# Three plain gate pairs instead of four in an FFN, and low halves written by adding DMAs

## The chip, the cores and the metric

One core of one Trainium2 chip runs the whole program in one launch. The metric is the device time of a launch in microseconds (us). TensorE is called PE below, its weight loads PEld, VectorE DVE, ScalarE ACT, GpSimd POOL, SyncE SP. ACT, POOL and SP can also issue DMAs.

## The reference, cut to what matters

The program is one inference step of a two-layer decoder for 512 prompt positions and 8 x 4 sample positions, 544 columns in all. Each layer has a half-step FFN, a mixer, a cross-attention and a second half-step FFN. The change concerns the four FFNs alone:

```
def _swiglu(x, wg, wu, wd):
    return (jax.nn.silu(x @ wg) * (x @ wu)) @ wd

x = x + 0.5 * _swiglu(_rmsnorm(x, n[0]), P['f1_wg'][l], P['f1_wu'][l], P['f1_wd'][l])
...
x = x + 0.5 * _swiglu(_rmsnorm(x, n[3]), P['f2_wg'][l], P['f2_wu'][l], P['f2_wd'][l])
```

x has 1024 features, the hidden layer 2816, all in float32.

## The kernel before

**Halves.** The kernel wants more precision than one matmul in PE's fast float32 format (fp32r) gives. So every operand is split: hi is the value rounded to fp32r by an ACT copy, lo is value minus hi, by a DVE subtraction. A product is three matmuls: hi weights by hi x, hi weights by lo x, lo weights by hi x (`TERMS`). In `dense` each is done for two halves of 272 columns, so the fifth matmul of a product is the first that reads the lo weights.

**Plain gates and pairs.** The 2816 hidden columns are 11 blocks ("pairs") of 256. A pair's product can be done in two ways. The plain way is two gates (`gate`) of 8 x 3 x 2 = 48 matmuls. The other way is a 2 x 2 block scheme with seven products instead of eight (`p1` to `p7` in `run`, 7 x 4 x 3 = 84 matmuls); it needs sums of weight blocks (the tile `sb` is made by two plain loads on SP and one adding DMA on POOL, in `sums`; `ga_s` makes two more sums on DVE), and sums and differences of x (`forms`). A group of products needs its own split weights: al (for p1 and p2), be (p5, p7), ga (p6, p3), de (p4), made by functions such as `al_h` (ACT copy) and `al_l` (DVE subtraction).

**Stages of an FFN.** In part 0 of three, the gate matrix `wg` of pairs 0 to 3 is done by eight plain gates, while DVE and ACT make the x forms; then `wu` of the same pairs by the seven products; then the partial down projection. Parts 1 and 2 do `wg` and `wu` both by the seven products. The plain gates work on x before its normalisation, whose factor `rstd` is multiplied in when a gate is evicted from PSUM (tile g); the forms need the normalised x, so they can't begin until `rstd` is there. Four calls of `forms`, one for each two chunks of x, follow gates 2, 3, 4 and 5.

**Order.** It is written out by hand: `step` collects functions, and `emit_steps` calls them one after the other; each engine runs its own instructions in that order. Ahead of a step, `conv` makes the split weights for up to the third gate in the list (`la=3`), from a raw buffer (two of these, `rawp`) into a wc buffer (three, `wcp`). When the last unit of a raw buffer is converted, `release` calls `issue`, which lets SP load the next block. The preparation of the first pair (`prelude`) stands ahead of the last gate. In the first FFN (`hold`), the first two gates start before anything else of the program and the factor comes after gate 1; in the others it comes after gate 0.

Two places in the code carry the rest. The conversion's DVE part, and the order in part 0:

```
        def low():
            tt(pool if u.on_pool else dve, w[:, 1], src, w[:, 0].bitcast(F32), ALU.subtract)
            if not u.raw:
                release(u)
...
                    if c == 7:
                        step(lambda P=items[0]: prelude(P))
                    step(lambda u, c=c: gate(u, c), us[j])
                    if c in (2, 3, 4, 5):
                        step(lambda kp=c - 2: forms(kp))
```

`actv` (L92), `tt` (L86), `stt` (L89) and `mm` (L95) are helpers, so many instructions carry one of these line numbers; the matmuls of the seven products carry L391.

Of the kernel before, what the change touches and what calls it, by code (L numbers as in the profile page):

```python
# [7 lines left out]
F32 = mybir.dt.float32  # L8
F32R = mybir.dt.float32r
AF = mybir.ActivationFunctionType  # L10
ALU = mybir.AluOpType
# [18 lines left out]
class Unit:  # L30
    def __init__(self, blk, k0, nk, c0, nc):
        self.blk, self.k0, self.nk, self.c0, self.nc = blk, k0, nk, c0, nc
        self.on_pool = self.late = self.raw = self.manual = False


class Block:
# [12 lines left out]
def trunk_kernel(ctx, tc, I, O):  # L49
    nc = tc.nc  # L50
    pe, act, dve, pool, sp = nc.tensor, nc.scalar, nc.vector, nc.gpsimd, nc.sync
# [11 lines left out]
    def nm(s):  # L63
        cnt[0] += 1
        return f"{s}{cnt[0]}"
# [10 lines left out]
    def P2(n="ps"):  # L76
        return PS(n), PS(n)
# [4 lines left out]
    def ph(ps, i):  # L82
        return ps[i][:, 0:HT]

    def tt(e, out, a, b, op):
        e.tensor_tensor(out=out, in0=a, in1=b, op=op)  # L86
# [4 lines left out]
    def actv(out, a, f, **kw):  # L91
        act.activation(out=out, in_=a, func=f, **kw)  # L92
# [13 lines left out]
    def step(fn, *units, la=3, ahead=None):  # L106
        steps.append((fn, units, la, ahead))
# [18 lines left out]
    def emit_steps():  # L126
        order = []
        for _, us, _, _ in steps:
            order.extend(us)
        blks = []  # L130
        for u in order:
            if u.blk not in blks[-3:]:
                blks.append(u.blk)
        st = {"dma": 0, "conv": 0}

        def issue(part=0):
            if part:
                b = blks[0]
                h = b.nk // 2
                sp.dma_start(out=b.tile[:, h:], in_=b.ap[:, h:])  # L140
                return
            if st["dma"] >= len(blks):
                return
            b = blks[st["dma"]]
            st["dma"] += 1
            b.tile = rawp.tile([128, b.nk, b.nc], F32, tag="raw", name=nm("raw"))
            if b.extra:
                sp.dma_start(out=b.tile, in_=b.ap)
                b.extra(b)
            elif st["dma"] == 1:  # L150
                h = b.nk // 2
                sp.dma_start(out=b.tile[:, 0:h], in_=b.ap[:, 0:h])
            else:
                sp.dma_start(out=b.tile, in_=b.ap)

        def release(u):
            u.blk.left -= 1
            if u.blk.left == 0:
                issue()

        def conv(defer=None):
            u = order[st["conv"]]
            st["conv"] += 1
            if u.manual:
                return
            w = wcp.tile([128, 2, u.nk, u.nc], F32R, tag="wc", name=nm("wc"))
            src = u.blk.tile[:, u.k0:u.k0 + u.nk, u.c0:u.c0 + u.nc]
            actv(w[:, 0], src, AF.Copy)
            u.tile = w

            def low():
                tt(pool if u.on_pool else dve, w[:, 1], src, w[:, 0].bitcast(F32), ALU.subtract)
                if not u.raw:
                    release(u)
            if defer is None or not u.late:
                low()
            else:
                defer.append(low)

        S["release"] = release  # L180
        startup(C_NORM, issue, conv)
        used = 0
        for fn, us, la, ahead in steps:
            used += len(us)
            flush()
            post = []
            while ahead is not None and st["conv"] < min(len(order), used + ahead):
                conv()
            while us and st["conv"] < min(len(order), used - len(us) + la):
                conv(post)  # L190
            fn(*us)
            for f in post:
                f()
            for u in us:
                if u.raw:
                    release(u)
        while later or waiting:
            flush()
# [15 lines left out]
    def split(hi, lo, src, delay=True):  # L214
        actv(hi, src, AF.Copy)

        def f():
            tt(dve, lo, src, hi.bitcast(F32), ALU.subtract)
        if delay:
            later.append(f)  # L220
        else:
            f()

    def sumsq(c):
        if c == 0:
# [68 lines left out]
    def ffn(which, l, next_g, tail=None):  # L294
        wg, wu = I[which + "_wg"][l], I[which + "_wu"][l]
        gcol = C_NORM + (l * 4 + (3 if which == "f2" else 0)) * 8
        G, XF, hh, hl = {}, {}, {}, {}
        hold = l == 0 and which == "f1"
        held = []
        kmap = [(z, 2 * (z % 4) + 1 - z // 4) for z in (4, 0, 5, 1, 6, 2, 7, 3)]  # L300

        def gate(u, c):
            ps = P2("gps")
            dense(ps, u, xh, xl, kmap)
            held.append((ps, c))
            if c == 7:
                for k in range(KD):
                    xh[k] = xl[k] = None
            if hold and c == 0:
                return  # L310
            if c == int(hold):
                norm_end()
            for ps, c in held:
                for i in range(2):
                    if c % 2 == 0:
                        G[c // 2, i] = U([128, 2, HT], n="g")
                    tt(dve, G[c // 2, i][:, c % 2], ph(ps, i), hb(S["rstd"], i), ALU.mult)
                if c % 2:
                    for i in range(2):
                        actv(G[c // 2, i], G[c // 2, i], AF.Silu)  # L320
            held.clear()
            if c == 7:
                S["rstd"] = S["ss"] = None

        def forms(kp):
            xs = D([128, 2, NT], n="xs")
            v = xs.rearrange("p a (h t) -> p (a h) t", h=2)
            t1, t2 = U([128, 2, HT], n="xt"), U([128, 2, HT], n="xt")
            b = U([128, 2, HT], F32R, n="xb")
            hs, ls = ([U([128, 2, HT], F32R, n="xf") for z in range(3)] for y in range(2))  # L330
            for j in range(2):
                stt(xs[:, j], x[2 * kp + j], col(gcol + 2 * kp + j), S["rstd"], ALU.mult, ALU.mult)
            actv(b[:, 0], v[:, 0], AF.Copy)
            actv(hs[0], v[:, 2:4], AF.Copy)
            tt(dve, t1, v[:, 0:4:3], v[:, 1:2].to_broadcast([128, 2, HT]), ALU.subtract)
            actv(hs[1], t1, AF.Copy)
            stt(t2[:, 0], t1[:, 0], -1.0, v[:, 3], ALU.mult, ALU.subtract)
            tt(dve, b[:, 1], v[:, 0], b[:, 0].bitcast(F32), ALU.subtract)
            stt(t2[:, 1], t2[:, 0], -1.0, v[:, 2], ALU.mult, ALU.subtract)
            actv(hs[2], t2, AF.Copy)  # L340
            for z, src in enumerate((v[:, 2:4], t1, t2)):
                tt(dve, ls[z], src, hs[z].bitcast(F32), ALU.subtract)
            XF[1, kp] = (b[:, 0], b[:, 1])
            for i, z, a in ((2, 0, 0), (3, 0, 1), (5, 1, 0), (7, 1, 1), (6, 2, 0), (4, 2, 1)):
                XF[i, kp] = (hs[z][:, a], ls[z][:, a])
# [119 lines left out]
        def pair(w, p, up):  # L465
            src = w[p]
            blk = Block(src[:, 0:12])
            P = blk.unit(0, 12, 0, 128)
            P.manual, P.up, P.p = True, up, p

            def sums(b):
                P.sb = D([128, 8, 128], n="sb")
                for z in range(2):
                    sp.dma_start(out=P.sb[:, 4 * z:4 * z + 4], in_=src[:, 12:16])
                pool.dma_start(out=P.sb, in_=src[:, 4:12], accum_op=ALU.add)
            blk.extra = sums
            return P
# [23 lines left out]
        for part, (p0, np) in enumerate(((0, 4), (4, 4), (8, 3))):  # L501
            prs = range(p0, p0 + np)
            if part == 0:
                items = [pair(wu, p, True) for p in prs]
                for p in prs:
                    blk = Block(wg[p])
                    us = [blk.unit(8 * j, 8, 0, 128) for j in range(2)]
                    for j in range(2):
                        c = 2 * p + j
                        if c == 7:  # L510
                            step(lambda P=items[0]: prelude(P))
                        step(lambda u, c=c: gate(u, c), us[j])
                        if c in (2, 3, 4, 5):
                            step(lambda kp=c - 2: forms(kp))
            else:
                items = [pair(w, p, w is wu) for p in prs for w in (wg, wu)]
                step(lambda P=items[0]: prelude(P))
                step(last[0], last[1])
# [19 lines left out]
            us = []  # L538
# [1489 lines left out]
```

## Time and profile before

| | |
|---|---|
| median of 3 runs | 2382.9 us (2381.37 to 2384.38) |
| the profiled execution, whole | 2385.29 us |
| its span, first to last instruction | 2383.4 us |
| mean granted TensorE clock | 0.995 |
| DMA traffic | 325.37 MB, mean 137 GB/s |
| first gates of the four FFNs at | 7.02, 944.42, 1316.30, 1995.96 us of the span |
| POOL idle ahead of adding DMAs, waiting for the plain loads of a `wu` pair's sb | 295.6 us, 25 times |

A page of the profile gives busy time by engine, queues and groups of equal instructions; the chain of waits follows back from the last instruction what released each; a timeline lists instructions in order of time (start, us, engine, line, operation, tiles out<-in, count, and in brackets the idle time of the engine just ahead and what ended it). Starts of a timeline are in us from the span's start. Tile names have lost their numbers. Matmuls are pipelined: the busy time of one reaches into the next, so the distance of starts is what one costs.

### The profile page before, as it was taken

The page shows a single profiled execution, that of the slowest core. Times are in us where ns is not written, and L with a number is a line of the kernel's source. Part 1 is how long each engine was busy: PE and PEld are TensorE (multiplying, and loading weights), DVE is VectorE, ACT ScalarE, POOL GpSimd, SP SyncE. Part 2 cuts the span into 40 slices and gives each one's busy share as a digit, 9 for nine tenths or more (in the row PEclk, how much of TensorE's full clock was granted, in tenths as well). Part 3 has the DMA queues.
Part 4 walks back from the last instruction along what each step waited for, and adds up shares of the span by engine and source line. Part 5 has one row for each costly group of instructions (what it writes and reads, how often), then busy time and mean ns, then how long its engine had stood idle before and what let it go on. Part 6 is the DMA issues. An engine that isn't in the chain of part 4 may idle for free.

```text
span 2383.4 us, 46953 instructions
## 1 busy us (share of the span) xinstructions
PE 2348.4 (99%) x20030; PEld 2285.7 (96%) x20030; DVE 1493.3 (63%) x2371; ACT 1072.1 (45%) x1783; POOL 294.8 (12%) x315
## 2 busy tenths in 40 slices
PE   8999999998999999999999999999999999999998
PEld 8999999998889989999999999999999989999998
DVE  8757466658666655856556875646455656847474
ACT  6435245624545344534444543534443444525253
POOL 1000001244222003000001000001212002000001
PEclk9999999999999999999999999999999999999999
DMA  4446354223445471445454345544322552436452
GB/s 164 124 134 172 115 142 139 87 83 120 142 156 189 163 286 66 117 142 140 141 139 122 105 134 146 155 127 119 131 94 78 211 214 86 128 123 172 134 142 78
DMA packets 100306, 325.37 MB, mean 137 GB/s; under 512 B 18528, under 2 KB 25696, under 8 KB 86272
## 3 DMA queue, kind: packets, MB, share of 16 engines
q1 hardware_dynamic: 76000, 262.60, 31.3%
q0 software_dynamic: 10368, 37.75, 9.4%
q10 hardware_dynamic: 13728, 22.01, 2.7%
q8 instruction: 157, 2.57, 0.4%
q14 instruction: 53, 0.43, 0.1%
HBM read 310.10 MB, written 12.23 MB: 135 GB/s over the span
## 4 chain that ended last, share of the span: by engine, by line
PE 84%; DVE 10%; DMA 2%; ACT 2%; issue 1%; POOL 0%; ACTq 0%; SPq 0%; DVEq 0%; POOLq 0%
PE dps L95 21%; PE wA L391 17%; PE wC L391 8%; PE wo L95 8%; PE wB L391 4%; PE q L95 4%; PE vp L95 4%; PE gps L95 3%; PE pA L95 2%; DVE wc L86 2%; PE kp L95 2%; PE pB L95 1%; DVE xf L86 1%; PE up L95 1%; PE sc L95 1%
## 5 line engine op out<-in xcount | busy, mean ns | idle before, releaser
L86 DVE TENSOR_TENSOR wc<-raw,wc 128x1024 fp32r<-128x1024 f32 (+1 forms) x306 | 379.4, 1245 | 266.2 <-ACT wc L92 265.2
L95 PE MATMUL dps<-hid,wc 128*128 128x272 f32 x4224 | 534.9, 288 | 0.6 <-DVE wc L86 0.6
L95 PEld LDWEIGHTS dps<-hid,wc 128*128 128x128 f32 x4224 | 531.4, 188 | 1.3 <-DVE wc L86 1.2
L92 ACT ACTIVATE wc<-raw 128x1024 fp32r<-128x1024 f32 (+1 forms) x322 | 331.0, 1032 | 249.0 <-PE dps L95 201.2
L89 DVE SCALAR_TENSOR_TENSOR x<-dps,x 128x272 f32<-128x272 f32 x192 | 75.6, 434 | 221.2 <-PE dps L95 221.2
L95 PE MATMUL gps<-xd,wc 128*128 128x272 f32 x1344 | 177.4, 291 | 7.7 <-ACT xd L92 7.0
L95 PEld LDWEIGHTS gps<-xd,wc 128*128 128x128 f32 x1344 | 173.0, 190 | 8.5 <-ACT xd L92 7.0
L92 ACT ACTIVATE wc<-sb 128x1024 fp32r<-128x1024 f32 x72 | 76.0, 1056 | 107.5 <-DMA sb<-in_f_wg_dram 44.3
L391 PE MATMUL wC<-xf,wc 128*128 128x272 f32 x864 | 121.0, 288 | 2.1 <-DVE wc L86 2.0
L391 PE MATMUL wA<-xf,ga 128*128 128x272 f32 x864 | 120.6, 289 | 1.7 <-ACT q L92 1.7
L391 PE MATMUL wA<-xb,wc 128*128 128x272 f32 x864 | 120.7, 289 | 1.5 <-DVE wc L86 1.5
L391 PE MATMUL wA<-xf,de 128*128 128x272 f32 x864 | 120.4, 288 | 0.0
L391 PE MATMUL wC<-xf,ga 128*128 128x272 f32 x864 | 120.1, 288 | 0.0
L391 PE MATMUL wA<-xf,wc 128*128 128x272 f32 x864 | 120.1, 288 | 0.0
L391 PE MATMUL wB<-xf,wc 128*128 128x272 f32 x864 | 119.7, 287 | 0.0
L391 PEld LDWEIGHTS wC<-xf,wc 128*128 128x128 f32 x864 | 113.0, 188 | 2.9 <-DVE wc L86 2.9
L391 PEld LDWEIGHTS wA<-xf,ga 128*128 128x128 f32 x864 | 113.1, 188 | 2.5 <-ACT q L92 2.5
L391 PEld LDWEIGHTS wA<-xb,wc 128*128 128x128 f32 x864 | 113.1, 188 | 1.9 <-DVE wc L86 1.7
L391 PEld LDWEIGHTS wA<-xf,de 128*128 128x128 f32 x864 | 113.1, 188 | 0.0
L391 PEld LDWEIGHTS wA<-xf,wc 128*128 128x128 f32 x864 | 113.0, 188 | 0.0
L391 PEld LDWEIGHTS wC<-xf,ga 128*128 128x128 f32 x864 | 112.9, 188 | 0.0
L391 PEld LDWEIGHTS wB<-xf,wc 128*128 128x128 f32 x864 | 112.7, 188 | 0.0
(367 smaller groups left out, 4362.9 us busy)
## 6 DMA issues: line engine op xcount, KB each, us to landing
raw<-in_f_wu_dram SPq DMA_DIRECT2D x44, 768.0 KB, 4.3
sb<-in_f_wu_dram SPq DMA_DIRECT2D x88, 256.0 KB, 4.7
sb<-in_f_wu_dram POOLq DMA_DIRECT2D x44, 512.0 KB, 5.4
raw<-in_f_wg_dram SPq DMA_DIRECT2D x28, 768.0 KB, 4.2
raw<-in_f_wda_dram SPq DMA_DIRECT2D x16, 1024.0 KB, 4.8
raw<-in_f_wdb_dram SPq DMA_DIRECT2D x16, 1024.0 KB, 4.8
sk<-in_kcT_dram SPq DMA_DIRECT2D x32, 512.0 KB, 7.4
sv<-in_vc_dram SPq DMA_DIRECT2D x64, 256.0 KB, 6.9
```

Source lines behind the costliest of these rows:

```text
L86: e.tensor_tensor(out=out, in0=a, in1=b, op=op)
L89: dve.scalar_tensor_tensor(out=out, in0=a, scalar=s, in1=b, op0=op0, op1=op1)
L92: act.activation(out=out, in_=a, func=f, **kw)
L95: pe.matmul(out=out, lhsT=l, rhs=r, start=start, stop=stop)
L391: pe.matmul(out=bank[:, 0:HT], lhsT=w(p)[:, kp], rhs=XF[i, kp][xx], start=first and kp == 0 and j == 0, stop=kp == 3 and j == 2, skip_grou ...
```

## The change

In every FFN but the first, three pairs of `wg` are plain gates (`plain`), and the fourth pair of part 0 is done by the seven products, ahead of its `wu` pair. The forms move with it: they follow gates 1 to 4, and `prelude` stands ahead of gate 5. In all four FFNs the lo halves of the plain gates' weights (all but the first two gates of the first FFN) and of three of the x forms are no longer made by DVE: ACT writes -hi into the lo half, and a DMA issued by POOL adds the value to it, from DRAM for the weights and from SBUF for the forms. The raw buffer of such a unit is released as soon as ACT has copied it.

```diff
     def __init__(self, blk, k0, nk, c0, nc):
         self.blk, self.k0, self.nk, self.c0, self.nc = blk, k0, nk, c0, nc
-        self.on_pool = self.late = self.raw = self.manual = False
+        self.on_pool = self.late = self.raw = self.manual = self.by_dma = False
...
             u.tile = w
+            if u.by_dma:
+                lo_by_dma(w[:, 1], w[:, 0], u.blk.ap[:, u.k0:u.k0 + u.nk, u.c0:u.c0 + u.nc])
+                release(u)
+                return
...
+    def lo_by_dma(lo, hi, src):
+        actv(lo, hi.bitcast(F32), AF.Copy, scale=-1.0)
+        pool.dma_start(out=lo, in_=src.bitcast(F32R), accum_op=ALU.add)
...
         hold = l == 0 and which == "f1"
+        plain = 4 if hold else 3
...
-            if c == 7:
+            if c == 2 * plain - 1:
                 for k in range(KD):
                     xh[k] = xl[k] = None
...
-            if c == 7:
+            if c == 2 * plain - 1:
                 S["rstd"] = S["ss"] = None
...
             for z, src in enumerate((v[:, 2:4], t1, t2)):
-                tt(dve, ls[z], src, hs[z].bitcast(F32), ALU.subtract)
+                lo_by_dma(ls[z], hs[z], src)
...
-                items = [pair(wu, p, True) for p in prs]
-                for p in prs:
+                items = [pair(w, p, w is wu) for p in prs for w in (wg, wu) if w is wu or p >= plain]
+                for p in range(plain):
                     blk = Block(wg[p])
                     us = [blk.unit(8 * j, 8, 0, 128) for j in range(2)]
                     for j in range(2):
                         c = 2 * p + j
-                        if c == 7:
+                        us[j].by_dma = c > 1 or not hold
+                        if c == 2 * plain - 1:
                             step(lambda P=items[0]: prelude(P))
                         step(lambda u, c=c: gate(u, c), us[j])
-                        if c in (2, 3, 4, 5):
-                            step(lambda kp=c - 2: forms(kp))
+                        if 0 <= c - plain + 2 < 4:
+                            step(lambda kp=c - plain + 2: forms(kp))
```

Three places of the order, all in the second FFN (layer 0, f2). First ACT after the eviction of gates 0 and 1 (g is their Silu; raw1336 holds the weights of gates 4 and 5; xb and xf are forms). Before:

```order
L92 ACTIVATE g1353_11200<-g1353_11200 128x544
L92 ACTIVATE wc1358_11261<-raw1336_11066 128x1024
L92 ACTIVATE xb1366_11321<-xs1363_11318 128x272
L92 ACTIVATE xf1367_11322<-xs1363_11318 128x544
L92 ACTIVATE xf1368_11323<-xt1364_11319 128x544
L92 ACTIVATE xf1369_11324<-xt1365_11320 128x544
L92 ACTIVATE wc1373_11341<-raw1336_11066 128x1024
```

Gate 4's weights (wc1358) are copied ahead of the first forms, gate 5's (wc1373) behind them. The same place of the change:

```order
L92 ACTIVATE g1353_11221<-g1353_11221 128x544
L92 ACTIVATE xb1362_11290<-xs1359_11287 128x272
L92 ACTIVATE xf1363_11291<-xs1359_11287 128x544
L92 ACTIVATE xf1364_11292<-xt1360_11288 128x544
L92 ACTIVATE xf1365_11293<-xt1361_11289 128x544
L92 ACTIVATE xf1366_11294<-xf1363_11291 128x544
L92 ACTIVATE xf1367_11295<-xf1364_11292 128x544
L92 ACTIVATE xf1368_11296<-xf1365_11293 128x544
L92 ACTIVATE wc1369_11313<-raw1336_11086 128x1024
L92 ACTIVATE wc1369_11313<-wc1369_11313 128x1024
```

Gate 4's weights (wc1369) have moved behind the first forms and their three negations, and have a negation of their own.

Second ACT from the last forms to the first pair's weights (al from raw, be from sb). Before, where the last forms follow gate 5 and gates 6 and 7 are still to come:

```order
L92 ACTIVATE xb1411_11573<-xs1408_11570 128x272
L92 ACTIVATE xf1412_11574<-xs1408_11570 128x544
L92 ACTIVATE xf1413_11575<-xt1409_11571 128x544
L92 ACTIVATE xf1414_11576<-xt1410_11572 128x544
L92 ACTIVATE wc1422_11647<-raw1374_11344 128x1024
L92 ACTIVATE wc1423_11649<-sb1375_11346 128x1024
```

Al's and be's copies stand right behind the third form. With the change, where the last forms follow gate 4 and only gate 5 is still to come:

```order
L92 ACTIVATE xb1406_11544<-xs1403_11541 128x272
L92 ACTIVATE xf1407_11545<-xs1403_11541 128x544
L92 ACTIVATE xf1408_11546<-xt1404_11542 128x544
L92 ACTIVATE xf1409_11547<-xt1405_11543 128x544
L92 ACTIVATE xf1410_11548<-xf1407_11545 128x544
L92 ACTIVATE xf1411_11549<-xf1408_11546 128x544
L92 ACTIVATE xf1412_11550<-xf1409_11547 128x544
L92 ACTIVATE wc1413_11567<-raw1355_11227 128x1024
L92 ACTIVATE wc1414_11569<-sb1356_11229 128x1024
```

Three negations have come in ahead of al's copy.

Third POOL's DMAs of the gate stage with the change (wc: weights of a gate, from DRAM; xf: forms; sb: the weight sums of the first pair). Before, only the sb were there:

```order
L230 DMA wc1346_11157<-in_f2_wg_dram 128x1024
L230 DMA wc1354_11223<-in_f2_wg_dram 128x1024
L484 DMA sb1356_11229<-in_f2_wu_dram 128x1024
L230 DMA xf1366_11294<-xs1359_11287 128x544
L230 DMA xf1367_11295<-xt1360_11288 128x544
L230 DMA xf1368_11296<-xt1361_11289 128x544
L230 DMA wc1369_11313<-in_f2_wg_dram 128x1024
L230 DMA xf1381_11378<-xs1374_11371 128x544
L230 DMA xf1382_11379<-xt1375_11372 128x544
L230 DMA xf1383_11380<-xt1376_11373 128x544
L230 DMA wc1384_11397<-in_f2_wg_dram 128x1024
L484 DMA sb1386_11403<-in_f2_wu_dram 128x1024
```

POOL runs them in this order, so a wait of sb1356 for its plain loads holds back the first forms, and gate 4's weights (wc1369) stand behind three forms.

## The prediction

> **What bounds the kernel now.** I read the page first, then the chain of waits around one of the FFNs that change, then the timelines of PE, ACT and DVE in its gate stage.
>
> ```profile
> span 2383.4 us, 46953 instructions
> ...
> PE 2348.4 (99%) x20030; PEld 2285.7 (96%) x20030; DVE 1493.3 (63%) x2371; ACT 1072.1 (45%) x1783; POOL 294.8 (12%) x315
> ...
> PE 84%; DVE 10%; DMA 2%; ACT 2%; issue 1%; POOL 0%; ACTq 0%; SPq 0%; DVEq 0%; POOLq 0%
> ```
>
> PE is the bound: fewer matmuls help one for one, and any wait that PE takes on costs one for one. The 10% of DVE in the chain have to be read by stage. In the second FFN (layer 0, f2) the chain has these pieces (start, us, what):
>
> ```profile
> 944.42 6.03 PE gps L95 x48
> ...
> 1001.76 3.01 PE wA L391 x24
> ...
> 1012.28 3.01 PE wA L391 x24
> ```
>
> A gate (48 matmuls) takes 6.03 us; one seven-product pair (84) comes every 1012.28 - 1001.76 = 10.52 us. The PE timeline where gates end and products begin:
>
> ```profile
> 993.38 1.65 PE L391 MATMUL wA<-xb,wc 128*128 128x272 f32 x12
> 994.87 1.68 PE L391 MATMUL wC<-xf,wc 128*128 128x272 f32 x12
> 996.98 1.78 PE L391 MATMUL wA<-xf,ga 128*128 128x272 f32 x12 [0.43 <-ACT q L92]
> ```
>
> Only the third product (p6) waits, by 996.98 - 993.38 - 3.01 = 0.6 us. So here the DVE of the chain runs beside a PE that is fed in time; it is late, but just not late enough. The first FFN is different:
>
> ```profile
> 54.07 1.65 PE L95 MATMUL gps<-xd,wc 128*128 128x272 f32 x11 [0.63 <-DVE wc L86]
> ...
> 61.84 1.52 PE L391 MATMUL wA<-xb,wc 128*128 128x272 f32 x10 [1.52 <-DVE wc L86]
> ...
> 64.42 1.52 PE L391 MATMUL wC<-xf,wc 128*128 128x272 f32 x10 [0.82 <-DVE wc L86]
> 66.36 1.79 PE L391 MATMUL wA<-xf,ga 128*128 128x272 f32 x12 [0.41 <-ACT q L92]
> ```
>
> There PE really waits for DVE's lo halves. Both stages in one view (PE, PEld, DVE, ACT, POOL busy):
>
> ```profile
> 944.25:996.98 52.73, 52.30 (x414) 51.92 (x413) 45.43 (x72) 29.37 (x43) 3.13 (x3) 1.00 0.38 110
> ...
> 22.45:66.36 43.91, 40.53 (x315) 39.45 (x313) 40.71 (x64) 24.77 (x37) 1.89 (x2) 1.00 0.38 109
> ```
>
> DVE is nearly full, ACT has half its time free and POOL nearly all. The change moves work in that direction; what decides is not the sum but the order on ACT and the time until a DMA lands.
>
> **PE work.** In three FFNs two gates go (12.06 us) and one pair comes (10.52): -1.5 us each, -4.6 in all.
>
> **The new wait at gate 4.** These rows give the durations (ACT and DVE timelines, ACT groups, DMA issues):
>
> ```profile
> 951.79 1.05 ACT L92 ACTIVATE wc<-raw 128x1024 fp32r<-128x1024 f32 x1
> ...
> 957.42 0.78 DVE L86 TENSOR_TENSOR g<-gps,rstd 128x272 f32<-128x272 f32 x2
> 963.33 0.79 DVE L86 TENSOR_TENSOR g<-gps,rstd 128x272 f32<-128x272 f32 x2 [2.03 <-PE gps L95]
> ...
> 967.48 0.66 ACT L92 ACTIVATE xf<-xt 128x544 fp32r<-128x544 f32 x1 [0.52 <-DVE xt L89]
> 968.04 1.05 ACT L92 ACTIVATE wc<-raw 128x1024 fp32r<-128x1024 f32 x1
> ...
> L92 ACT ACTIVATE xf<-xt 128x544 fp32r<-128x544 f32 x8 | 5.3, 661 | 2.5 <-DVE xt L89 2.1
> ...
> raw<-in_f_wu_dram SPq DMA_DIRECT2D x44, 768.0 KB, 4.3
> sb<-in_f_wu_dram SPq DMA_DIRECT2D x88, 256.0 KB, 4.7
> sb<-in_f_wu_dram POOLq DMA_DIRECT2D x44, 512.0 KB, 5.4
> ```
>
> The x forms of one index run from DVE's eviction g to the end of the third ACT copy: 968.14 - 963.33 = 4.81 us. With three gate pairs the first forms follow gate 1, whose eviction starts at 957.42, and the conversion of gate 4's weights stands behind them on ACT. So: third copy done 962.2; three negations (0.66 us, a new one every 0.55) 964.0; copy and negation of the weights, each waiting for the one ahead, 2 x 1.05: 966.1; the adding DMA, priced as the existing adding DMA of the same 512 KB, nearest possible row, at 5.3: **971.4**. Counting back from 993.38, gate 4's first matmul is due at 993.38 - 4 x 6.03 = 969.26, and its fifth, the first to read lo, at 969.8. PE waits at least 1.6 us. Before, this lo half was one DVE pass of 1.2 us.
>
> How adding DMAs share is not in the trace, since two never overlap. Bounds come from the queues:
>
> ```profile
> q1 hardware_dynamic: 76000, 262.60, 31.3%
> q0 software_dynamic: 10368, 37.75, 9.4%
> ...
> 976.46 0.89 POOL L475 DMA_DIRECT2D sb<-in_f_wu_dram  x1 [28.59 <-DVE xf L86]
> ```
>
> q0 is the adding ones: 9.4% of 2383.4 us over 72 of them is 3.1 us of all 16 engines for 512 KB. A form (272 KB, from SBUF) takes by bytes 1.65 us of that; at the plain rate of q1 (31.3% for 262.6 MB) 0.8. I take 1.2, the middle, since its source is not HBM and no row has it; an unshared form then lands 5.3 - 1.9 = 3.4 us after issue. If they go one after the other: the pair's sb, moved ahead of the forms on POOL, has its loads released by the copy of gate 3's weights (951.79 in the row; gate 2's negation ahead of it puts its end at 953.9); the second goes out at 954.8 and lands 4.7 later, at 959.5, and sb itself at 964.9; the forms, issued 0.89 us apart from 962.9, at 966.3, 967.5, 968.7; gate 4's lo at 968.7 + 3.1 = 971.8: **2.0 us late**. With 0.8 for a form it stays 1.6; with 1.65 it is 3.4.
>
> **The new wait at p1.** The last forms now stand right before the preparation of the first pair, one gate ahead of p1 and not two. The rows of the same preparation before:
>
> ```profile
> 991.16 1.22 DVE L86 TENSOR_TENSOR wc<-raw,wc 128x1024 fp32r<-128x1024 f32 x1
> ...
> 993.75 1.22 DVE L86 TENSOR_TENSOR wc<-sb,wc 128x1024 fp32r<-128x1024 f32 x1
> ```
>
> From al's lo (991.16) through the sums, be's lo (993.75), gate 7's eviction, two Silu and the copy q to p6 (996.98) pass 5.82 us. DVE, relieved of 1.9 us of form lows and 1.2 of weight lows a gate, evicts gate 4 at once: 963.33 + 2 x 6.03 = 975.4, plus gate 4's lateness L. Then forms 4.81, negations 1.75, al's copy 1.05, and 5.82: p6 at 988.8 + L; after one more pair the same point of the program as before's 996.98 is 999.4 + L. So each of the three FFNs loses 2.4 + L us, the -1.5 of PE and the old 0.6 included. A late gate 5 (its lo lands some 0.5 to 2 us late by the same steps) is absorbed: ACT's chain hangs on gate 4's end, not on gate 5's. With L = 2.0: +4.4 each, **+13.1** for three.
>
> **The first FFN** keeps four pairs, and only its lo halves move.
>
> ```profile
> 18.29 1.99 ACT L92 ACTIVATE wc<-raw 128x1024 fp32r<-128x1024 f32 x2
> ...
> 16.89 3.28 POOL L86 TENSOR_TENSOR sq<-sq,sq 128x544 f32<-128x544 f32 x2 [0.34 <-ACT sq L92]
> ...
> 22.45 1.74 PE L95 MATMUL gps<-xd,wc 128*128 128x272 f32 x11
> ```
>
> Gate 2's weights: copy 18.29 to 19.34, negation to 20.4 (POOL is free from 20.2), landing 25.7; needed at 22.95: 2.75 late. Gate 5: eviction of gate 2 at 31.3, then 4.81 + 1.75 + 2.1 to the issue at 40.0; landing behind three forms 45.7, needed 43.8: 1.9 late. Then POOL stands at the first pair's sb (its loads go out only after gate 5's copy and land at 44.6), the next forms and gate 6's lo queue behind it (49.9, 51.1, 52.3, 53.5, 56.6), needed 51.7: 4.9. Gate 7, by the same: 0.7. In exchange the three DVE waits go: without any wait p6 starts at 22.45 + 6 x 6.03 + 3.01 = 61.65; with 10.25 of new ones at 71.9, against 66.36: **+5.5**. Ends: +3.3 with 0.8 for a form, +8.6 with 1.65.
>
> **Sum.** 13.1 + 5.5 = +18.6 us; ends 12.0 + 3.3 = +15 and 3 x 5.8 + 8.6 = +26. The profiled execution took 2385.29, its span 2383.4, the median of the runs is 2382.9; the sum is a difference, so I put it on the median: 2401.5, from 2398 to 2409. The other stages keep their order; the extra pair runs as the four others do, which show no wait. About 0.2% (4.8 us) is what a measurement of this kernel can tell from no change.
>
> **Rivals.**
> *Adding DMAs do not queue on each other* (15%): gate 4's lo stays at 971.4 (L = 1.6, 3 x 4.0 = 12.0) and the first FFN has 2.75 + 1.5 + 2.1 late, p6 at 68.0: +1.6. Together +13.6: 2396.5. For it: the engines are busy only 38% in the stage. Against: 3.1 + 3 x 1.2 = 6.7 us of engine time a gate of 6.03. [...]
> *They land in time* (15%; the case that is not slower). It decides at gate 4: landing within 969.8 - 966.1 = 3.7 us of issue makes L = 0. Price: 3 x 2.4 = +7.1 from ACT alone, and -4.7 in the first FFN once its waits for DVE are gone (61.65 against 66.36): +2.4, 2385, within 0.2%. For it: a plain load of 768 KB lands in 4.3 us, so it is the adding that costs, and only for sb is that cost known. Against: 44 issues of the same size and kind with a median of 5.4. [...]
> *ACT is in time too* (6%): then PE alone counts, -4.6 and the three 0.6 at p6, -4.7 in the first FFN: -11, 2372. It would need al's copy 4.5 us earlier than the order on ACT allows.
> *More than the sum* (14%): weight loads of the plain queue slow the adding ones, or POOL's waits for sb hold the forms past p5; over 2409.
>
> **Chances.** The forecast 50%, the rest as above. The range 2385 to 2410 leaves out the 6% below and the 14% above. Faster by over 0.2%: 6%; within: 14% (nearly all of "in time"); slower: 80%.
>
> **What would show it.** Right: PE waits of some 2 us at gate 4's fifth matmul for the DMA wc, of about 2 us at p1 for ACT and DVE wc, and about 2.75 at gate 2 of the first FFN; landings near 5.3 alone and 6 or more behind forms. Wrong: gate 4 without a wait (landing under 3.7), p1 without one (the negations not ahead of al's copy in time), or forms on q0 that take far less than 1.2 us, which brings the result to +14 or below.

## The result, and the profile after

The changed kernel takes 2448.8 us (median; 2447.5 to 2450.2), the kernel before on the same chip 2383.6: ratio 1.027, 95% interval 1.0257 to 1.0283. The loss is 65.1 us where 18.6 was forecast, and beyond the range. The profile page of the changed kernel (span; engines; the adding queue; the chain by engine; two groups of matmuls):

```profile
span 2448.5 us, 47158 instructions
...
PE 2363.1 (97%) x19994; PEld 2298.7 (94%) x19994; DVE 1445.9 (59%) x2308; ACT 1129.0 (46%) x1873; POOL 360.6 (15%) x390
...
q0 software_dynamic: 21168, 65.28, 15.3%
...
PE 82%; DMA 7%; DVE 6%; ACT 2%; issue 1%; POOL 1%; SPq 0%; ACTq 0%; DVEq 0%; POOLq 0%
...
L95 PE MATMUL gps<-xd,wc 128*128 128x272 f32 x1092 | 161.6, 311 | 49.0 <-DMA wc<-in_f_wg_dram 41.9
...
L400 PE MATMUL wC<-xf,wc 128*128 128x272 f32 x900 | 128.0, 290 | 14.2 <-DMA xf<-xt 10.8
```

The chain shows what took over: DVE fell from 10% to 6%, DMA rose from 2% to 7%. Two groups hold it: the gates wait 41.9 us for lo halves of weights, p5 waits 10.8 us for forms. And PE is busy 14.7 us longer, with 36 matmuls fewer. The windows view of the changed kernel, over the gate stage and first products of the second FFN and of the first, shows two things that were not there before (us; busy time of PE, PEld, DVE, ACT, POOL; granted clock; share of DMA time; GB/s):

```profile
965.00:1025.00 60.00, 48.88 (x349) 48.05 (x349) 30.71 (x49) 37.39 (x57) 17.37 (x20) 0.91 0.83 175
...
22.00:87.00 65.00, 42.97 (x295) 42.15 (x295) 25.86 (x44) 34.13 (x50) 16.73 (x20) 0.82 0.82 173
```

Before, the clock in these stages was 1.00 and the DMA share 0.38; now the clock is 0.91 and 0.82, and the share 0.83 and 0.82. The PE timeline of the changed kernel, at the waits of the first FFN (three rows) and of the second:

```profile
30.34 6.45 PE L95 MATMUL gps<-xd,wc 128*128 128x272 f32 x38 [6.67 <-DMA wc<-in_f_wg_dram]
...
57.55 6.49 PE L95 MATMUL gps<-xd,wc 128*128 128x272 f32 x38 [7.47 <-DMA wc<-in_f_wg_dram]
...
73.17 7.13 PE L95 MATMUL gps<-xd,wc 128*128 128x272 f32 x38 [7.89 <-DMA wc<-in_f_wg_dram]
...
996.55 6.34 PE L95 MATMUL gps<-xd,wc 128*128 128x272 f32 x38 [5.02 <-DMA wc<-in_f_wg_dram]
1002.73 0.41 PE L95 MATMUL gps<-xh,wc 128*128 128x272 f32 x2
...
1006.49 6.48 PE L95 MATMUL gps<-xd,wc 128*128 128x272 f32 x38 [2.35 <-DMA wc<-in_f_wg_dram]
...
1020.22 0.82 PE L400 MATMUL wC<-xf,wc 128*128 128x272 f32 x2 [3.76 <-DMA xf<-xt]
```

These are gates 2, 5 and 6 of the first FFN, then gates 4 and 5 and p5 of the second. Each x38 is the rest of a gate behind the wait. From 996.55 to 1002.73 are 6.18 us for 38 matmuls, which at the old pace (6.03 us for 48) take 4.77: after this wait PE also ran slower for a while, 1.4 us in all.

A measure for the four FFNs is the time from the first gate matmul to the first matmul of part 0's down projection, read from the PE timelines:

| stage, us | FFN 1 | FFN 2 | FFN 3 | FFN 4 |
|---|---|---|---|---|
| before | 97.06 | 90.41 | 90.56 | 90.47 |
| after | 120.49 | 104.58 | 104.30 | 102.68 |
| difference | +23.4 | +14.2 | +13.7 | +12.2 |

That is 63.6 of the 65.1 us that separate the spans. Counted from the starts of PE's matmuls in these stages: waits (gaps over 0.3 us) grew from 6.8 to 57.2 us; matmuls at the slow pace (0.227 us from start to start instead of 0.1255) grew from 21 to 192, which is 17 us; the PE work that went is 4.6 us. Sum 62.8. By FFN the slow pace is 4 to 5 us in each.

Why the lo halves come so late shows in three views of the second FFN. ACT's and POOL's timelines of the changed kernel, around gate 4's weights:

```profile
985.23 1.05 ACT L92 ACTIVATE wc<-raw 128x1024 fp32r<-128x1024 f32 x1
986.31 1.06 ACT L92 ACTIVATE wc<-wc 128x1024 fp32r<-128x1024 f32 x1
...
983.68 0.86 POOL L484 DMA_DIRECT2D sb<-in_f_wu_dram  x1 [7.02 <-DMA sb<-in_f_wu_dram]
...
987.67 0.86 POOL L230 DMA_DIRECT2D wc<-in_f_wg_dram  x1 [0.47 <-ACT wc L92]
...
1007.20 0.87 POOL L484 DMA_DIRECT2D sb<-in_f_wu_dram  x1 [12.65 <-DVE xt L89]
1007.73 1.22 POOL L230 DMA_DIRECT2D xf<-xs  x1
```

and the DMA issues of this stretch (queue; count; KB each; median us from issue to landing): the first pair's plain loads of sb, gate 4's adding DMA, the second pair's plain load, and the x forms and second sb loads of 985 to 1012 us:

```profile
sb<-in_f_wu_dram SPq DMA_DIRECT2D x2, 256.0 KB, 6.4
...
wc<-in_f_wg_dram POOLq DMA_DIRECT2D x1, 512.0 KB, 8.8
...
raw<-in_f_wu_dram SPq DMA_DIRECT2D x1, 768.0 KB, 9.3
...
xf<-xt POOLq DMA_DIRECT2D x8, 272.0 KB, 9.2
...
sb<-in_f_wu_dram SPq DMA_DIRECT2D x2, 256.0 KB, 11.9
```

Before, the same plain loads took 4.3 and 4.7 us; here, beside adding DMAs, they took 9.3 and 6.4 to 11.9. Gate 4's adding DMA took 8.8 behind three forms, where sb's of the same 512 KB took 5.4 before. POOL works in order: from 994.6 to 1007.20 it stands at the second pair's sb, whose slowed plain loads it needs, and the three forms behind it, whose negations ended at 998.1, stand with it. Then sb, these three forms and three more, as soon as ACT has them, go out within 3.3 us. They land one after another, sb at 1012.74 and the first three forms at 1014.10, 1015.45 and 1016.82, and p5 waits until 1020.22 for the fifth form, which landed at 1020.17. (The trace gives POOL's wait to DVE's xt. But POOL goes on 0.58 us behind the landing of the later plain load, at 1006.62, as it did at the first sb, 0.56 us behind 983.12; so the load is what it waited for.)

### The profile page after: what moved, and what is told of

It reads as the page before. It is cut to its first block, busy times and chain, and to the rows that moved or that the text cites. A ratio compares the mean times of both kernels' runs of the same rounds, so it can differ in the third digit from the quotient of the medians.

```text
span 2448.5 us, 47158 instructions
## 1 busy us (share of the span) xinstructions
PE 2363.1 (97%) x19994; PEld 2298.7 (94%) x19994; DVE 1445.9 (59%) x2308; ACT 1129.0 (46%) x1873; POOL 360.6 (15%) x390
## 4 chain that ended last, share of the span: by engine, by line
PE 82%; DMA 7%; DVE 6%; ACT 2%; issue 1%; POOL 1%; SPq 0%; ACTq 0%; DVEq 0%; POOLq 0%
PE dps L95 20%; PE wA L400 17%; PE wC L400 9%; PE wo L95 8%; PE wB L400 4%; PE vp L95 4%; PE q L95 4%; DMA sb<-in_f_wu_dram 3%; PE gps L95 3%; PE pA L95 2%; PE kp L95 2%; DMA xf<-xt 1%; PE pB L95 1%; DMA wc<-in_f_wg_dram 1%; DVE wc L86 1%
## 5 line engine op out<-in xcount | busy, mean ns | idle before, releaser
L86 DVE TENSOR_TENSOR wc<-raw,wc 128x1024 fp32r<-128x1024 f32 (+1 forms) x279 | 347.3, 1250 | 278.8 <-ACT wc L92 278.2
L95 PE MATMUL gps<-xd,wc 128*128 128x272 f32 x1092 | 161.6, 311 | 49.0 <-DMA wc<-in_f_wg_dram 41.9
L95 PEld LDWEIGHTS gps<-xd,wc 128*128 128x128 f32 x1092 | 155.8, 209 | 51.8 <-DMA wc<-in_f_wg_dram 44.1
L400 PE MATMUL wC<-xf,wc 128*128 128x272 f32 x900 | 128.0, 290 | 14.2 <-DMA xf<-xt 10.8
L484 POOL DMA_DIRECT2D sb<-in_f_wg_dram x31 | 26.8, 864 | 692.9 <-DVE wc L86 318.3
L400 PE MATMUL wA<-xf,ga 128*128 128x272 f32 x900 | 127.5, 292 | 0.0
L400 PE MATMUL wB<-xf,wc 128*128 128x272 f32 x900 | 126.9, 291 | 0.0
L400 PE MATMUL wA<-xf,wc 128*128 128x272 f32 x900 | 125.3, 289 | 0.0
L400 PEld LDWEIGHTS wA<-xf,ga 128*128 128x128 f32 x900 | 120.0, 193 | 0.0
L400 PEld LDWEIGHTS wB<-xf,wc 128*128 128x128 f32 x900 | 119.6, 191 | 0.0
```

Of the source, the lines that this page charges most:

```text
L95: pe.matmul(out=out, lhsT=l, rhs=r, start=start, stop=stop)
L400: pe.matmul(out=bank[:, 0:HT], lhsT=w(p)[:, kp], rhs=XF[i, kp][xx], start=first and kp == 0 and j == 0, stop=kp == 3 and j == 2, skip_grou ...
```

## The experiments

Times of the kernel before on the same chip: 2387.1 us beside the first four runs, 2385.2 us beside all others. The stage differences below are against the profiled execution of the kernel before, as in the table.

**One part at a time.** First, three pairs but all lo halves on DVE:

```diff
-                lo_by_dma(ls[z], hs[z], src)
+                tt(dve, ls[z], src, hs[z].bitcast(F32), ALU.subtract)
...
-                        us[j].by_dma = c > 1 or not hold
+                        us[j].by_dma = False
```

> The pair half of the change alone: three plain gate pairs in all but the first FFN, every low half by DVE as before. Theory A (the adding DMAs and what queues on them make the loss): no adding DMA beside sb is left, so 2378 to 2386, the -4.6 of PE work less small waits. Theory B (three gate pairs are too few to cover the x forms, whoever makes the lows): DVE takes 7.07 us a gate step as in the trace before (963.33 to 970.40), the last forms end at 984.5 and not at 981.4, p1 waits some 4 us for al's low half and the three FFNs lose 4 to 5.5 us each: 2395 to 2400. Theory C (the negations on ACT and their order): none are left, as A.

Measured: 2400.2 us, ratio 1.0060 (1.0045 to 1.0075); stages 0.0, +3.8, +4.4, +3.3. Second, the DMAs with four gate pairs everywhere:

```diff
-        plain = 4 if hold else 3
+        plain = 4
```

> The DMA half alone: four plain gate pairs everywhere, low halves of gate weights and forms by negation and adding DMA. The first FFN is that of the changed kernel (23.4 us longer there to its down projection). Theory A: the other three get the same load of adding DMAs with one gate pair more, so they lose 10 to 20 us each, 2437 to 2467. Theory B: with four pairs the cover is back, the other three lose 0 to 3 each, 2405 to 2415. Theory C (ACT order alone, DMAs landing 5.3 us after issue): gates 5 and 6 wait 1.5 to 2 us each, 2415 to 2422.

Measured: 2466.4 us, ratio 1.0337 (1.032 to 1.0354); stages +23.7, +18.4, +21.3, +19.6. So the lo halves by negation and DMA cost far more than the missing cover of two gates, and with four pairs they cost more than with three. Third, weights by DMA and forms on DVE (the first edit of the first diff alone):

> The change with the forms' low halves back on DVE, so that only the gate weights' are added by DMA: 2.5 us of the engines a gate and none of 1.35. Theory A: the queue has room, the weights land 5.4 to 7 us after issue; gate 2 of the first FFN still waits 6.8 us beside a plain load, the later ones wait 0 to 3: 2395 to 2415. Theory C: ACT loses three of its five negations a gate, most of the loss goes too: 2390 to 2400. Theory B: 2 to 4 us in each FFN remain from the forms on DVE.

Measured: 2403.2 us, ratio 1.0069 (1.0048 to 1.009); stages +13.6, +2.2, +2.0, +1.1. Fourth, forms by DMA and weights on DVE (the second edit alone):

> The change with the gate weights' low halves back on DVE, so that only forms are added by DMA: 3 x 1.35 = 4.1 us of the engines a gate of 6.03. Theory A: it fits, gates do not wait; the last forms land behind the second pair's sb and p5 waits 0 to 4 us: 2385 to 2400. Theory C: the forms' three negations stay ahead of al's copy and of the weights' copies, so p1 still waits about 2.5 us in the three FFNs and gate 4 is at most 1 us late: 2390 to 2400; the two differ in the trace (PE waits for DMA xf, or for ACT and DVE wc at p1).

Measured: 2444.4 us, ratio 1.0244 (1.0228 to 1.0259); stages +13.3, +12.8, +13.2, +11.2. That is beyond every time in the expectation. In FFNs 2 to 4 the weights' DMAs alone are no cost: with them the stage is 1.6 to 2.4 us shorter than with three pairs alone. The forms' negations and DMAs are nearly the whole of the loss there. In the first FFN each half costs 13 us. PE's timeline of the forms-by-DMA kernel (start of p1, and p5, in the second FFN) and POOL's:

```profile
999.98 0.59 PE L400 MATMUL wA<-xb,wc 128*128 128x272 f32 x2 [4.53 <-ACT wc L92]
...
1010.84 0.82 PE L400 MATMUL wC<-xf,wc 128*128 128x272 f32 x2 [4.36 <-DMA xf<-xt]
...
997.43 0.86 POOL L484 DMA_DIRECT2D sb<-in_f_wu_dram  x1 [9.23 <-DMA sb<-in_f_wu_dram]
```

Two prices stand here side by side: p1 waits for ACT's copy of al, behind the forms' negations, and p5 for a form that stood behind sb on POOL.

**The place of sb on POOL.** The changed kernel, with the second pair's adding DMA issued behind the last forms:

```diff
...
+                if P.behind and len(pend) == 0 and not XF.get("done"):
+                    pend.append(add)
+                else:
+                    add()
...
```

(`behind` is set for the second pair of part 0 alone, `add` is its adding DMA, and a step behind the last `forms` calls what lies in `pend`.)

> The changed kernel, with only the second pair's adding DMA into sb put on POOL behind the last forms instead of ahead of them. Head-of-queue theory (POOL stands at that sb for its late loads, and six form DMAs wait behind it): forms(2) go out near 998 and forms(3) near 1009 in the second FFN, no longer at 1007 to 1010; p5 does not wait for a form (3.9 us before), the first FFN's last waits (8.05 at gate 6) shrink by half; 5 to 8 us less per FFN, 2420 to 2430 us in all. Bandwidth theory (the queue behind POOL is full whatever the order): forms land as late, over 2440 us.

Measured: 2436.6 us, ratio 1.0217 (1.0203 to 1.0231), 12 us less than the changed kernel; stages +25.8, +8.6, +9.6, +7.9. POOL's timeline of this kernel, where forms(2) and forms(3) go out (its stage starts 3.05 us later than the changed kernel's):

```profile
1000.33 0.86 POOL L230 DMA_DIRECT2D xf<-xs  x1 [2.73 <-ACT xf L92]
...
1011.16 0.86 POOL L230 DMA_DIRECT2D xf<-xs  x1 [8.18 <-ACT xf L92]
```

In the changed kernel forms(2) went out at 1007.73; here, 10.4 us earlier by the stage's own time, and p5 waits no more: 4.2 to 5.6 us gained in each of FFNs 2 to 4. In the first FFN, where the expectation had half of the last waits go, nothing was gained (2.3 us lost), and so the total missed the expected 2420 to 2430. In FFNs 2 to 4 standing at the second sb is about a third of the loss, not all.

**ACT's negations without the DMA.** The forms-by-DMA kernel, with DVE doing the addition:

```diff
-                lo_by_dma(ls[z], hs[z], src)
+                actv(ls[z], hs[z].bitcast(F32), AF.Copy, scale=-1.0)
+                tt(dve, ls[z], src, ls[z].bitcast(F32), ALU.add)
```

> The kernel with three pairs and the forms' lo halves by DMA (weights' on DVE, 2444 us), with DVE doing the addition in place of the DMA while ACT's negation stays. ACT-order theory (the negations ahead of al's copy cost p1 its 4.7 us): p1 still waits 4 us or more in each of the three FFNs, 2410 to 2420 us. Queue theory (only the DMAs cost): as three pairs with all lo halves on DVE, 2400 us, and the first FFN without a loss.

Measured: 2425.0 us, ratio 1.0168 (1.0154 to 1.0182), 25 us over three pairs alone, and beyond the 2420 of the expectation; stages +6.3, +9.3, +8.6, +9.9. PE's timeline of this kernel at p1, and DVE's at two successive evictions of gates and a scaling of x:

```profile
993.72 0.82 PE L401 MATMUL wA<-xb,wc 128*128 128x272 f32 x2 [7.80 <-ACT wc L92]
...
970.42 0.78 DVE L86 TENSOR_TENSOR g<-gps,rstd 128x272 f32<-128x272 f32 x2
971.12 1.47 DVE L89 SCALAR_TENSOR_TENSOR xs<-x,cols,rstd 128x544 f32<-128x544 f32 x2
...
978.99 0.78 DVE L86 TENSOR_TENSOR g<-gps,rstd 128x272 f32<-128x272 f32 x2
```

p1 waits 7.8 us, as the ACT-order theory has it, but by more: with DVE waiting for the negations and ACT for DVE, one index of forms takes 978.99 - 970.42 = 8.6 us, longer than a gate of 6.03. In the forms-by-DMA kernel DVE doesn't wait for the negations, so its p1 waited 4.5. Of the two prices above, p1's is therefore ACT's, and it needs no DMA.

**Plain loads beside adding DMAs.** The changed kernel, with gate weights' adding DMA reading the raw tile in SBUF, which is therefore given back, and reloaded, only after the landing:

```diff
-                lo_by_dma(w[:, 1], w[:, 0], u.blk.ap[:, u.k0:u.k0 + u.nk, u.c0:u.c0 + u.nc])
+                lo_by_dma(w[:, 1], w[:, 0], src)
```

> The changed kernel, with the adding DMA of a gate's weights reading the tile that already lies in SBUF instead of HBM; that tile is given back only when the lo half has landed, so the plain load that follows no longer runs beside it. Contention theory (a plain load beside an adding DMA is what makes it land after 9 us instead of 5.3): gate 2's lo in the first FFN lands at most 5.5 us after its issue, its wait falls from 6.8 to about 3 us, and the lo of gate 4 in the second FFN lands within 6.5 us. The total gains less, since the plain loads start later: 2435 to 2450 us. Rival (an adding DMA slows by itself, by what it does at the destination): landings as before, 9 us.

Measured: 2470.9 us, ratio 1.0363 (1.0347 to 1.0378); stages +21.5, +19.4, +21.7, +20.1. The DMA issues for gates 2 and 4 of the first FFN, in the changed kernel:

```profile
wc<-in_f_wg_dram POOLq DMA_DIRECT2D x1, 512.0 KB, 9.2
...
wc<-in_f_wg_dram POOLq DMA_DIRECT2D x1, 512.0 KB, 5.3
```

and for gate 2 in this one:

```profile
wc<-raw POOLq DMA_DIRECT2D x1, 512.0 KB, 4.7
```

So contention was right about the landing, 4.7 us instead of 9.2 with no plain load beside it (the source differs too; but gate 4's DMA from DRAM, beside which nothing ran, landed after 5.3). It was wrong about the total and about gate 4 of the second FFN, whose DMA landed 9.9 us after its issue and not within 6.5. The timelines of this kernel, POOL's first sb and gate 4's DMA behind it, and PE's wait:

```profile
986.03 0.86 POOL L484 DMA_DIRECT2D sb<-in_f_wu_dram  x1 [10.69 <-DVE xs L89]
...
988.18 2.24 POOL L230 DMA_DIRECT2D wc<-raw  x1
...
998.10 6.32 PE L95 MATMUL gps<-xd,wc 128*128 128x272 f32 x38 [7.89 <-DMA wc<-raw]
```

The raw tile comes free later, so the pair's plain loads start later, POOL stands longer at sb, and everything behind it moves: a second sign that POOL's order costs, by making it worse. (Here too the trace names a DVE instruction; that it was the plain load again is the author's estimate, from the 0.56 and 0.58 us of the changed kernel.) How adding DMAs share with no plain load beside them shows in the first FFN of the changed kernel, from 65.99 us on, where the last plain load had landed: sb, three forms and a gate's weights, issued from 58.25 to 60.39, landed at 66.57, 67.89, 69.25, 70.67 and 73.13. So they went one after the other, a form every 1.3 to 1.4 us and the weights after 2.5.

**GpSimd instead of DVE.** The kernel before, with the lo halves of gates 4 to 7 subtracted on POOL (`us[j].on_pool = c > 3`):

> The kernel before (four gate pairs, no DMA for lo halves), with the lo halves of gates 4 to 7 made by GpSimd's subtraction instead of DVE's. If DVE's length is what the waits of the first FFN come from (0.8, 1.5 and 0.8 us) and the 0.6 at p6 of the others: 3 to 6 us less than the kernel before. If GpSimd's subtraction (2.4 us and more) is late itself or slows DVE while it runs: within 3 us of the kernel before, or slower.

Measured: 2395.2 us, ratio 1.0041 (1.0029 to 1.0054); stages +1.2, +2.4, +2.9, +4.0. The timelines of this kernel, DVE and POOL at the same moment, and PE:

```profile
46.09 4.32 DVE L89 SCALAR_TENSOR_TENSOR xs<-x,cols,rstd 128x544 f32<-128x544 f32 x2
...
47.16 2.66 POOL L86 TENSOR_TENSOR wc<-raw,wc 128x1024 fp32r<-128x1024 f32 x1
...
49.87 6.57 PE L95 MATMUL gps<-xd,wc 128*128 128x272 f32 x38 [2.09 <-POOL wc L86]
```

Two scalings of x take DVE 4.32 us here; in the kernel with the negations but DVE adding, where POOL subtracts nothing, the same pair takes 1.47 (the row at 971.12 above). The 2.85 us more are close to POOL's 2.66, as if DVE had stood still meanwhile. Two more such pairs of this kernel, at 38.70 and 54.88 us, took 2.93, so 1.46 more, with POOL subtracting until 1.64 and 1.65 us after their start. What holds DVE up, no run here shows.

**Order on ACT.** The changed kernel, with the next gate's copy and negation put ahead of the forms of the same step (`ahead=3` in the forms' `step`):

> The changed kernel, with the copy and negation of the next gate's weights put ahead of the forms of the same step on ACT, in all FFNs. ACT-order theory (gate 4's lo is late because its copy stands behind the forms and their negations): the DMA of gate 4 in the second FFN goes out some 6 us earlier, gate 4's 5.2 us and the first FFN's 7.6 at gate 5 mostly go, forms come 2 us later; 3 to 6 us less per FFN, 2425 to 2440 us. Queue theory (POOL's standing at sb and the landing times are all): the waits only move to the next gate or p5, within 6 us of the changed kernel.

Measured: 2436.3 us, ratio 1.0216 (1.0201 to 1.0231); stages +15.5, +10.4, +12.1, +11.8. PE's timeline of this kernel, second FFN:

```profile
994.64 5.04 PE L95 MATMUL gps<-xd,wc 128*128 128x272 f32 x38 [3.06 <-DMA wc<-in_f_wg_dram]
...
1005.12 0.82 PE L400 MATMUL wA<-xb,wc 128*128 128x272 f32 x2 [4.69 <-ACT wc L92]
```

Gate 4's wait is gone, as ACT's order said; gate 5 waits 3.06 instead of 2.35 and p1 4.69 instead of nothing, as the queue theory said. Only the first FFN gains much (7.9 us), the others 3.7, 1.6 and 0.5. The total lies in the range of ACT's order, but in the third and fourth FFN the gain is below the 3 to 6 us that it expects.

**A candidate.** Three pairs in FFNs 2 to 4, forms on DVE, only gates 3 to 5's weights by DMA there and copied ahead of the forms, the first FFN as before:

```diff
-                lo_by_dma(ls[z], hs[z], src)
+                tt(dve, ls[z], src, hs[z].bitcast(F32), ALU.subtract)
...
-                        us[j].by_dma = c > 1 or not hold
+                        us[j].by_dma = c > 2 and not hold
...
-                            step(lambda kp=c - plain + 2: forms(kp))
+                            step(lambda kp=c - plain + 2: forms(kp), ahead=None if hold else 3)
```

> A candidate: three plain gate pairs in the second to fourth FFN, with the lo halves of gates 3 to 5 there by adding DMA (copy and negation put ahead of the forms of the same step), all other lo halves by DVE, the first FFN as in the kernel before. If the loss of the three FFNs with weights by DMA (2.1, 2.0 and 1.2 us) comes from the late lo of gates 4 and 5 alone (0.5 and 2.0 us, and the lower clock behind them): these waits go, each of the three FFNs takes 0.5 to 2.5 us less than in the kernel before, 2378 to 2384 us where the kernel before has 2385. If DVE's forms set the pace whatever ACT does: p1 waits 1.5 us instead, within 2 us of the kernel before.

Measured: 2397.0 us, ratio 1.0045 (1.0031 to 1.0058); stages 0.0, +2.0, +1.0, +1.5. No gate waits, but p1 and p5 do, for DVE (0.89 and 0.81 us in the second FFN). The time is beyond both expectations. Of the 10.5 us between the spans only 4.5 stand in the stages. And with the forms one gate earlier (`c - plain + 3` for these FFNs):

> The same, with the forms of these three FFNs one gate earlier (behind gates 0 to 3 instead of 1 to 4). If DVE's order is what p1 waits for: 1 us less per FFN than without it, 2375 to 2381 us. If DVE is full from the norm's end on: the same as without it.

Measured: 2389.9 us, ratio 1.0021 (1.0013 to 1.003); stages +0.1, +0.7, -0.1, +0.6. PE's timeline of this kernel, its only waits in the gates and products up to the third pair:

```profile
969.28 5.04 PE L95 MATMUL gps<-xd,wc 128*128 128x272 f32 x38 [1.04 <-DMA wc<-in_f_wg_dram]
...
976.49 5.03 PE L95 MATMUL gps<-xd,wc 128*128 128x272 f32 x38 [0.92 <-DMA wc<-in_f_wg_dram]
```

p1 and p5 no longer wait, so DVE's order was what they waited for. That is worth 3.3 us in the four stages; the rest of the 7 us between the two medians lies outside them. It is less than the expectation's 2375 to 2381. Now the stages are nearly level with before: the 1.5 us of PE work and the old 0.6 at p6 pay for two short waits. It is the best version with three pairs, and still slower than before by 0.1 to 0.3%. Part of what remains lies behind the stage: part 2 of the second and third FFN takes 63.9 and 63.7 us up to its down projection, against 61.7 and 61.9 before. Why was not settled. It need not be the three pairs: in the kernel of 2397.0 us the first FFN, which is as before, took 63.5 us there instead of 62.0.

## Why the prediction was wrong

The sum had +5.5 us for the first FFN and +4.4 for each of the others; measured were +23.4, and +14.2, +13.7 and +12.2. What each step of it became:

- **PE work, -1.5 an FFN**: right in count (36 matmuls fewer), and buried. That three pairs give too little cover for the forms was right too: alone, with all lo halves on DVE, they lost 3.3 to 4.4 us an FFN. (The foreseen 2.4 with the DMAs in time is another sum: negations on ACT, and DVE relieved.)
- **ACT's order, issue of gate 4's DMA at 966.1**: right. That is 21.85 us behind the stage's start at 944.25; measured 987.67 - 965.83 = 21.84, and 21.83 in the fourth FFN; in the third, where gate 0 had waited 0.94 us, 23.05.
- **Gate 4's landing, L = 2.0**: this step failed. Gate 4 waited 5.0, 3.1 and 3.2 us in FFNs 2 to 4. The price of an adding DMA alone (5.3 us) held, and so did the queueing: from the rows below, a form issued at 58.78 lands at 67.9 and the weights issued at 60.39, third behind it, at 73.1, 5.2 us for two forms and the weights. What failed in the second FFN is the sentence on the pair's sb, "the second goes out at 954.8 and lands 4.7 later": that 4.7 is a plain load's price with no adding DMA beside it. The two loads took 5.0 and 7.7 us, and POOL stood at sb until 983.68, which is 17.85 us behind the stage's start and not the 15.25 of 959.5. That is 2.6 of the 3.0 us by which L was too small. I had priced the plain loads as if the change left them alone. In the fourth FFN this is not the cause: there the loads took 4.5 and 4.6 us and POOL went on after 14.78, but the three forms landed 23.5, 24.7 and 26.2 us behind the stage's start, where the sum has 22.05, 23.25 and 24.45 (966.3, 967.5 and 968.7). Why they took longer stays open.

POOL's timeline of the changed kernel for that reading, first FFN:

```profile
58.78 1.21 POOL L230 DMA_DIRECT2D xf<-xs  x1
...
60.39 2.28 POOL L230 DMA_DIRECT2D wc<-in_f_wg_dram  x1
```

its DMA issues, of the same two:

```profile
xf<-xs POOLq DMA_DIRECT2D x1, 272.0 KB, 9.1
...
wc<-in_f_wg_dram POOLq DMA_DIRECT2D x1, 512.0 KB, 12.7
```

and of the fourth FFN the first pair's plain loads of sb among the DMA issues, and gate 4's wait in PE's timeline:

```profile
sb<-in_f_wu_dram SPq DMA_DIRECT2D x2, 256.0 KB, 4.5
...
2077.36 6.57 PE L95 MATMUL gps<-xd,wc 128*128 128x272 f32 x38 [3.20 <-DMA wc<-in_f_wg_dram]
```

- **p1, 2.4 + L late**: wrong in place. The sum has 4.5 us of waits up to p6 beside L (2.4, the 1.5 of PE and the old 0.6). p1 did not wait. Instead gate 5 waited (I had called it absorbed) and p5 did, for a form of the row dammed up behind the second pair's sb, which the sum left out: 2.35 and 3.76 us in the second FFN, 2.67 and 3.76 in the third, 2.60 and 3.23 in the fourth. The experiment with that sb behind the forms puts 4.2 to 5.6 us an FFN on this sb. With weights on DVE, where no gate waits in the second FFN, a wait of that size is at p1 (4.53; among the signs it is about 2).
- **First FFN, waits of 2.75, 1.9, 4.9 and 0.7**: 6.67, 7.47, 7.89 and none. Same failed step: plain loads and adding DMAs were priced as if they did not meet. Gate 2's DMA was priced alone; the plain load that its own copy sets free runs beside it and makes 9.2 us of 5.3. Without that load it was 4.7, and the wait 2.14. Gate 5's DMA, issued at 46.24 beside three plain loads, took 11.3 us to land and not the summed 5.7, and the plain loads of the first sb 9.2 and 11.7 instead of some 4.7, so that POOL stood there until 58.25.
- **Rivals.** "More than the sum" (14%) is what happened, by both mechanisms that it named: plain loads slow the adding ones, and POOL's waits for sb hold the forms past p5. It was given too little. The prediction cites the DMA engines' busy share of 38% before as room; with the adding DMAs it was 82%. "Adding DMAs do not queue on each other" is settled the other way, by the landings one after another (66.57 to 73.13 us, above).
- **Not in the prediction at all**: the clock. 17 of the 63.6 us are matmuls at the slow pace behind waits. One such wait cost about 1.5 us more, a third to a half as much again in FFNs 2 to 4, where the waits are 2.4 to 5 us, and about a fifth in the first, where they are 6.7 to 7.9.

## What to carry to other kernels

A DMA that adds was no free vector instruction here: it kept the DMA engines busy twice as long per byte as a plain load (before: 9.4% of the span for 37.75 MB, against 31.3% for 262.60 MB), went one after the other with its like (a form landed every 1.3 to 1.4 us, a gate's weights 2.5 behind it), and sb's plain loads of 256 KB, on which the same queue then waited, took 6.4 to 11.9 us beside it instead of 4.7. So price it with its neighbours, those that its own release triggers first. POOL issued its DMAs in order, and an sb that waited for its loads held back forms that were ready; behind them it cost 4.2 to 5.6 us less in each of FFNs 2 to 4. So an instruction that waits for a load should not stand ahead of issues that are ready. To a forecast PE wait like the twelve of the changed kernel's stages, 2.35 to 7.89 us long, add some 1.5 us for the clock: three of them cost 4 to 5 us in each FFN.

## What was not expected of the hardware

**The clock after a wait.** In the changed kernel's third FFN a wait of 3.08 us is followed by matmuls 0.227 us apart instead of 0.1255; its row is below, and that of the kernel with weights by DMA, where it follows a wait of only 1.91. The row of the kernel with the copy ahead, shown above, has a wait of 3.06 without it: 38 matmuls in 5.04.

The PE timeline of the changed kernel:

```profile
1384.11 6.55 PE L95 MATMUL gps<-xd,wc 128*128 128x272 f32 x38 [3.08 <-DMA wc<-in_f_wg_dram]
```

and of the kernel with weights by DMA:

```profile
992.15 6.56 PE L95 MATMUL gps<-xd,wc 128*128 128x272 f32 x38 [1.91 <-DMA wc<-in_f_wg_dram]
```

In the changed kernel all twelve waits of 2.35 us or more in an FFN's stage were followed by it. The granted clock was 0.50 from 57 to 59 us, where gate 5's wait in the first FFN ends (57.55), and a matmul then took 0.227 us instead of 0.1255. The 16 slow matmuls behind the 3.08 us, 0.227 each, are 3.6 us. A wait of 1.91 us had it and one of 3.06 had not; what decides it, no run here shows.

**Adding DMAs and plain loads.** A plain load of 768 KB took 9.3 us beside adding DMAs, 4.3 otherwise; an adding DMA of 512 KB took 9.2 beside a plain load, 5.3 alone.

**POOL and DVE.** While a POOL subtraction of 2.66 us ran, two of DVE's scalings took 2.85 us longer.
